# A set amount of other work between the steps of a recurrence (one encoder layer, one core)

## The chip, the core and the metric

The kernel runs on one core of a Trainium2 chip. The metric is the device time of one execution in microseconds (us). TensorE (PE in the profile) multiplies matrices, VectorE (DVE) and ScalarE (ACT) work on elements, GpSimd (POOL) does small row statistics and issues some DMAs, SyncE (SP) issues the others. Each engine runs its own queue of instructions in order, and waits on semaphores for the others.

## The reference

One layer of an encoder on 512 positions of width 1024, in three sub-layers: token mixing, cross-attention into 256 memory tokens, and a gated MLP with a short convolution. Each has a norm before and after it and is added to the residual. The change is in the token mixing, which has two groups of heads side by side: eight attention heads, and four heads of a gated recurrence in both directions over the positions. Shortened, the recurrence is:

```python
def hgrn2_group(q, zf_fwd, zf_bwd, i_in, g, lb, out_g):
    f = lb + (1 - lb) * sigmoid(z)          # a forget gate per direction and key column
    k = 1 - f                               # and S = diag(f_t) S + k_t v_t, o_t = q_t S
    o = bidirectional_gated_scan(silu(q), log(f_fwd), log(f_bwd), v=i_in)
    return rmsnorm(o, out_g) * silu(g)      # per head of 128
mixed = concatenate([attention, recurrence]) @ w_out
```

## The kernel before

**Matmuls.** Nearly all products are made from three matmuls (`mm3`, lines 278 to 280): each operand is split into a rounded high part and a rest. Activations are kept as such pairs (`big`), weights come through `issue`: a load into `raw`, a high part `wh` (L222, ScalarE), and a rest `wl` (L224 on VectorE, or L229 on ScalarE and an accumulating DMA L230 from GpSimd's queue). A unit of weights is 1024 columns, of 24 matmuls of 512 columns.

**The recurrence** of head h (`hgrn_core`) is not a scan over positions. It fills a 512 by 128 table of the scores of every pair of positions within a block, level by level for m = 1, 2, 4, ... 64: L644 copies the keys into order (`kc`), L647 multiplies keys and queries of neighbouring blocks of m, L679 puts the result in its place under a mask, and L673 scales keys and queries, in place, by the decay over m, for the next level. L678 forms the decays of the next level. L636 is the first product (a position with itself), with the sum of keys of L629. Then come m = 128 (L654, copied by L681), the transposed keys for the state (L659, copied by L660), the state (L664, copied by L666), and the output of the head (L685 to L687). L691 squares the output, L296 and L297 turn the sums into a row factor on GpSimd, L697 scales and gates the output, and L701 transposes it for the output projection. All products of the recurrence are of 128 columns, plain float32, which PE does in two passes (a transpose in one). They go to the two banks `ps_c`.

**Streams.** `hgrn_core` and the projections are generators. `weave` asks that stream for its next step which is furthest behind its share of work; a step is worth the number that it yields, in us by the author's count (`MM`, 0.216 for a matmul of 512 columns), and a stream that yields None is passed over. There are three weaves:

- before the first, the input, the values `v` and head 0's projection are made;
- the first, of `mix_projections` (100) and `cores` (53): output gate, then q and gates of head 1, of head 2 (L577 to L607), the transposes of the normed memory (L317), the attention's q, k and v (bank `ps_s` and `ps_o`; norm and rotation L725 to L750, and transposes L780 and L757), and q and gates of head 3; beside it the recurrence of heads 0, 1 and 2, one after the other;
- the second, of head 3's recurrence (22), attention (46; scores L872, transposes L882, weighing L893) and memory keys and values (52).

A projection yields after two slices of the contraction, 6 x 0.216 = 1.30; the recurrence yields 1.0 after each level, and 3.0 after the statistics. In the first weave the shares would give a recurrence step of 1.0 for each 1.89 of projections.

**Order on the engines.** The framework that builds the program puts instructions of one engine past others where it takes their inputs to be late; so rows that one loop writes together can stand apart in the order of an engine. All quoted line numbers are those of the kernel before; in the changed kernel they are 14 to 16 higher.

Of the kernel before, what the change touches and what calls it, by code (L numbers as in the profile page):

```python
# [47 lines left out]
NEG_SCALAR = frozenset(range(9, 33))  # L48
NEG_POOL = frozenset(range(33, 42))
CORE_SHARE, ATT_LEAD = 53.0, 4.0  # L50
KEY_TURNS = {1: (0, 1), 2: (2, 3)}
WARM, SPREAD_STEP = 4, 2
LEVELS = (1, 2, 4, 8, 16, 32, 64)
# [5 lines left out]
def pat(t, off, dims):  # L59
    a = t[:]  # L60
    return bass.AP(tensor=a.tensor, offset=a.offset + off, ap=[list(a.ap[0])] + [list(d) for d in dims])
# [8 lines left out]
        return self.hi[kc // n][:, kc % n, sl], self.lo[kc // n][:, kc % n, sl]  # L70


def weave(*streams):
    live = [[g, 0.0, float(total)] for g, total in streams]
    while live:
        live.sort(key=lambda s: s[1] / s[2])
        for s in live:
            try:
                step = next(s[0])
            except StopIteration:  # L80
                live.remove(s)
                break
            if step is not None:
                s[1] += step
                break
        else:
            raise RuntimeError("no stream can go on")


def layer(tc, io, out):  # L90
# [14 lines left out]
    def small():  # L105
        return sm.tile([P, 16], F32, name="small", tag="small")

    def bank(tag):
        return ps.tile([P, 512], F32, name="ps_" + tag, tag=tag)

    def big(shape, dt=F32):
        return b8.tile(shape, dt, name="big", tag="big")

    def tmp2(shape=(P, 512), dt=F32, tag="ta"):
        return t2.tile(list(shape), dt, name="tmp2", tag=tag, bufs=TMP_BUFS[tag])
# [8 lines left out]
    def split_scaled(hi, lo, src, factor):  # L124
        nc.scalar.mul(hi, src, factor)
        nc.vector.scalar_tensor_tensor(out=lo, in0=src, scalar=factor, in1=hi.bitcast(F32), op0=ALU.mult,
                                       op1=ALU.subtract)
# [154 lines left out]
    def blk(b):  # L282
        return slice(b * P, (b + 1) * P)
# [10 lines left out]
    def rstd_of(ss, n, width, r=None):  # L294
        r = small() if r is None else r
        nc.gpsimd.tensor_scalar(r[:, :n], ss, 1.0 / width, EPS, op0=ALU.mult, op1=ALU.add)  # L296
        last_pow[0] = nc.gpsimd.tensor_tensor(out=r[:, :n], in0=r[:, :n], in1=nhalf[:, :n], op=ALU.pow).ins  # L297
        return r
# [267 lines left out]
    def pair(act, i):  # L566
        t = big([P, 2, 2, T], F32R)
        act.hi[i], act.lo[i] = t[:, 0], t[:, 1]
# [49 lines left out]
    def hgrn_core(h):  # L618
        while h not in heads:
            yield None  # L620
        q, qk, tt = heads[h]
        room = big([P, 2048])
        a = room[:, 0:1024].rearrange("p (s w n) -> p s w n", s=NB, w=2)
        kt = room[:, 1024:1536].rearrange("p (s n) -> p s n", s=NB)
        st = room[:, 1536:1792].rearrange("p (g n) -> p g n", g=2)
        diag = a[:, :, 0, :]
        ksum, kc, qc = [tmp2(tag="th") for _ in range(3)]
        nc.scalar.mul(ksum, qk[:, 1, 0, :], oml[:, 0, h:h + 1])
        nc.vector.scalar_tensor_tensor(out=ksum, in0=qk[:, 1, 1, :], scalar=oml[:, 1, h:h + 1], in1=ksum,  # L629
                                       op0=ALU.mult, op1=ALU.add)  # L630
        for side, to in ((1, kc), (0, qc)):
            (nc.vector.tensor_copy if (h, side) == (1, 0) else nc.scalar.copy)(
                to, pat(qk, side * 2 * T, [[2, T // 2], [T + 1, 2]]))
        o = bank("c").rearrange("p (b n) -> p b n", b=NB)
        for b in range(NB):
            nc.tensor.matmul(o[:, b, :], ksum[:, blk(b)], q[:, blk(b)], start=True, stop=True)  # L636
        nc.scalar.copy(diag, o)
        yield 1.0
        toff = 0
        for i, m in enumerate(LEVELS + (128, 256)):  # L640
            if m <= 64:
                if m > 1:
                    kc = tmp2(tag="th")
                    nc.scalar.copy(kc, pat(qk, 2 * T, [[2 * m, T // (2 * m)], [T + m, 2], [1, m]]))  # L644
                o = bank("c").rearrange("p (b n) -> p b n", b=NB)
                for b in range(NB):
                    nc.tensor.matmul(o[:, b, :], kc[:, blk(b)], qc[:, blk(b)] if m == 1 else  # L647
                                     pat(qk, b * P, [[2 * m, P // (2 * m)], [T + m, 2], [1, m]]),
                                     start=True, stop=True)
            elif m == 128:  # L650
                o = bank("c").rearrange("p (b n) -> p b n", b=NB)
                for sb in range(NB):
                    tb = sb ^ 1
                    nc.tensor.matmul(o[:, sb, :], qk[:, 1, sb % 2, blk(sb)], qk[:, 0, tb % 2, blk(tb)],  # L654
                                     start=True, stop=True)
            else:
                o = bank("c").rearrange("p (b n) -> p b n", b=NB)
                for sb in range(NB):
                    nc.tensor.transpose(o[:, sb, :], qk[:, 1, sb // 2, blk(sb)], ident)  # L659
                nc.scalar.copy(kt, o)  # L660
                yield 0.5
                o = bank("c")[:, :256].rearrange("p (g n) -> p g n", g=2)
                for sb in range(NB):
                    nc.tensor.matmul(o[:, sb // 2, :], kt[:, sb, :], v[:, sb, blk(h)],  # L664
                                     start=sb % 2 == 0, stop=sb % 2 == 1)
                nc.scalar.copy(st, o)  # L666
                yield 1.0
                break
            nblk = T // m
            npair = nblk // 2  # L670
            for s, off, gap in ((1, 1, nblk - 1), (0, nblk + 1, -(nblk + 1))):
                c = pat(qk, s * 2 * T, [[2 * m, npair], [T + m, 2], [1, m]])
                nc.vector.tensor_tensor(out=c, in0=c, in1=pat(tt, toff + off, [[2, npair], [gap, 2], [0, m]]),  # L673
                                        op=ALU.mult)
            if m < 128:
                src = tt[:, toff:toff + 2 * nblk].rearrange("p (i two) -> p two i", two=2)
                toff += 2 * nblk
                nc.vector.tensor_mul(tt[:, toff:toff + nblk], src[:, 0, :], src[:, 1, :])  # L678
                nc.vector.copy_predicated(diag, masks[:, i:i + 1, :].to_broadcast([P, NB, P]), o)  # L679
            else:  # L680
                nc.scalar.copy(a[:, :, 1, :], o)  # L681
            yield 1.0
        o = bank("c").rearrange("p (b n) -> p b n", b=NB)
        for tb in range(NB):
            nc.tensor.matmul(o[:, tb, :], a[:, tb, 0, :], v[:, tb, blk(h)], start=True, stop=False)  # L685
            nc.tensor.matmul(o[:, tb, :], a[:, tb ^ 1, 1, :], v[:, tb ^ 1, blk(h)], start=False, stop=False)
            nc.tensor.matmul(o[:, tb, :], qk[:, 0, tb // 2, blk(tb)], st[:, 1 - tb // 2, :], start=False, stop=True)  # L687
        on = tmp2((P, NB, P), tag="th")
        ss = small()
        for b in range(NB):  # L690
            nc.scalar.activation(on[:, b, :], o[:, b, :], ACT.Square, accum_out=ss[:, b:b + 1])  # L691
        r = rstd_of(ss[:, :NB], NB, P)
        yield 3.0
        while len(sg_box) < 1 + NB:
            yield None
        for b in range(NB):
            nc.vector.scalar_tensor_tensor(out=on[:, b, :], in0=o[:, b, :], scalar=r[:, b:b + 1],  # L697
                                           in1=sg_box[0][:, b, blk(h)], op0=ALU.mult, op1=ALU.mult)
        o = bank("c").rearrange("p (b n) -> p b n", b=NB)
        for b in range(NB):  # L700
            nc.tensor.transpose(o[:, b, :], on[:, b, :], ident)  # L701
        if h % 2 == 0:
            pair(mix, 2 + h // 2)
        split_scaled(*mix.get(4 + h, slice(0, T)), o.rearrange("p b n -> p (b n)"), og[:, 0:1])
        rec_done[0] += 1
        yield 0.5
# [127 lines left out]
    def cores():  # L834
        for h in range(3):
            yield from hgrn_core(h)

    for i, _ in enumerate(hgrn_in(0)):
        if i == SPREAD_STEP:
            spread_r()  # L840
    weave((mix_projections(), 100.0), (cores(), CORE_SHARE))

    kT, vv, qT = qkv["kT"], qkv["vv"], qkv["qT"]
# [87 lines left out]
    def attention_filler():  # L931
        kv["k"] = Act([None] * 2, [None] * 2)
        for c in range(8):
# [3 lines left out]
            for step in proj_fm(kv["m"], M, "b", put_kx(c)):  # L937
                yield step
                turned[0] = c > max(KEY_TURNS)
            for b in KEY_TURNS.get(c, ()):  # L940
                turn_k(b)
# [150 lines left out]
    us = [bank(up_tags[n]) for n in range(4)]  # L1092
# [254 lines left out]
```

## Time and profile before

| | |
|---|---|
| median of 3 runs | 816.31 us (816.14 to 816.73) |
| span of the profiled execution, first to last instruction | 813.8 us |
| granted TensorE clock, mean | 0.998 |
| PE busy | 803.3 us, 99% of the span |
| PE weight loads | 691.0 us, 85% |
| DVE busy | 574.7 us, 71% |
| ACT busy | 482.1 us, 59% |
| POOL busy | 136.9 us, 17% |
| first weave, about | 54 to 200 us |
| second weave, about | 200 to 306 us |

The profile is of one execution; its span lies 2.5 us under the median of the runs, which hold what comes before the first and after the last instruction too. "Idle before" in brackets is the time that an engine stood still ahead of an instruction, with what it waited for. A row "x8" stands for eight instructions in a row. Busy time of PE includes modelled ends, so that two matmuls overlap in the list; the distance of their starts tells the pace.

### The profile page before, as it was taken

To read this page: it belongs to the slowest core of one execution; us is meant where nothing else is said; L and a number is where in the kernel's file an instruction comes from. 1 tells how busy PE (TensorE), PEld (TensorE's weight loads), DVE (VectorE), ACT (ScalarE), POOL (GpSimd) and SP (SyncE) were. 2 spreads that over 40 slices of the span, in tenths; PEclk is the share of its full clock that TensorE was granted. 3 is DMA by queue.
4 is the path that set the end of the run, shared out by engine and by line. 5 is a ranking of instruction groups with operands and counts; after the bars stand their busy time and mean duration, and the time that the engine had idled before them with its cause. 6 is when DMAs were issued, how large, how long until landed. Compare 5 with 4: busy or idle time off the path is not lost.

```text
span 813.8 us, 11771 instructions
## 1 busy us (share of the span) xinstructions
PE 803.3 (99%) x4426; PEld 691.0 (85%) x4426; DVE 574.7 (71%) x868; ACT 482.1 (59%) x796; POOL 136.9 (17%) x213
## 2 busy tenths in 40 slices
PE   9999999999999999999999999999999999999996
PEld 7888888889998887888888898899999998888885
DVE  5456587469886865855453767987777788888765
ACT  5675757459988874644543553665555545566651
POOL 0111201053233102301010311211111111000301
PEclk9999999999999999999999999999999999999999
DMA  8685645569899753256634158776665677278852
GB/s 296 202 259 139 160 103 117 118 159 247 229 250 254 182 172 126 78 181 157 180 117 142 33 164 208 154 200 166 179 171 143 150 200 178 91 208 278 239 130 104
DMA packets 42457, 139.61 MB, mean 172 GB/s; under 512 B 5280, under 2 KB 6560, under 8 KB 42400
## 3 DMA queue, kind: packets, MB, share of 16 engines
q1 hardware_dynamic: 28944, 97.43, 35.5%
q0 software_dynamic: 12160, 38.54, 26.2%
q10 hardware_dynamic: 1296, 2.89, 1.0%
q8 instruction: 34, 0.56, 0.3%
q14 instruction: 23, 0.19, 0.1%
HBM read 135.17 MB, written 25.17 MB: 197 GB/s over the span
## 4 chain that ended last, share of the span: by engine, by line
PE 92%; DVE 3%; ACT 2%; issue 1%; POOL 1%; DMA 0%; DVEq 0%; POOLq 0%; SPq 0%; ACTq 0%
PE ps_b L279 10%; PE ps_b L280 10%; PE ps_b L278 10%; PE ps_s L278 6%; PE ps_s L280 6%; PE ps_s L279 6%; PE ps_o L278 5%; PE ps_o L279 5%; PE ps_o L280 5%; PE ps_c L278 5%; PE ps_c L280 5%; PE ps_c L279 5%; PE ps_c L647 3%; PE ps_o L893 2%; PE ps_s L872 2%; PE ps_o L882 2%
## 5 line engine op out<-in xcount | busy, mean ns | idle before, releaser
L222 ACT CAST wh<-raw 128x1024 fp32r<-128x1024 f32 x110 | 113.7, 1035 | 114.6 <-PE ps_b L279 35.3
L224 DVE TENSOR_TENSOR wl<-raw,wh 128x1024 fp32r<-128x1024 f32 (+1 forms) x77 | 92.3, 1201 | 72.2 <-ACT wh L222 72.0
L278 PE MATMUL ps_b<-big,wh 128*128 128x512 f32 (+1 forms) x344 | 122.3, 355 | 0.0
L280 PE MATMUL ps_b<-big,wl 128*128 128x512 f32 (+1 forms) x344 | 121.2, 352 | 0.0
L279 PE MATMUL ps_b<-big,wh 128*128 128x512 f32 (+1 forms) x344 | 121.2, 352 | 0.0
L280 PEld LDWEIGHTS ps_b<-big,wl 128*128 128x128 f32 x344 | 65.1, 189 | 8.5 <-DMA wl<-in_wu_dram 0.2
L278 PEld LDWEIGHTS ps_b<-big,wh 128*128 128x128 f32 x344 | 65.1, 189 | 8.3
L279 PEld LDWEIGHTS ps_b<-big,wh 128*128 128x128 f32 x344 | 65.1, 189 | 8.1
L673 DVE TENSOR_TENSOR big<-big 128x512 f32<-128x512 f32 x64 | 47.2, 755 | 9.6 <-PE ps_c L647 4.0
L278 PE MATMUL ps_s<-wh,big 128*128 128x512 f32 (+1 forms) x140 | 53.4, 383 | 0.0
L279 PE MATMUL ps_s<-wl,big 128*128 128x512 f32 (+1 forms) x140 | 53.3, 381 | 0.0
L280 PE MATMUL ps_s<-wh,big 128*128 128x512 f32 (+1 forms) x140 | 53.0, 379 | 0.0
L230 POOL DMA_DIRECT2D wl<-in_w_dram x33 | 29.3, 887 | 126.7 <-ACT wl L229 91.5
L122 DVE TENSOR_TENSOR big<-ps_o,big 128x512 fp32r<-128x512 f32 x54 | 36.9, 687 | 15.0 <-ACT big L121 13.4
L121 ACT CAST big<-ps_o 128x512 fp32r<-128x512 f32 x54 | 31.7, 588 | 18.5 <-PE ps_o L996 7.5
L278 PE MATMUL ps_s<-big,wh 128*128 128x256 f32 (+1 forms) x120 | 40.0, 334 | 0.0
L279 PE MATMUL ps_s<-big,wh 128*128 128x256 f32 (+1 forms) x120 | 40.0, 333 | 0.0
L280 PE MATMUL ps_s<-big,wl 128*128 128x256 f32 (+1 forms) x120 | 40.0, 333 | 0.0
L278 PE MATMUL ps_o<-wh,big 128*128 128x512 f32 (+1 forms) x102 | 39.2, 385 | 0.0
L279 PE MATMUL ps_c<-big,wh 128*128 128x256 f32 (+1 forms) x120 | 39.1, 326 | 0.0
L278 PE MATMUL ps_c<-big,wh 128*128 128x256 f32 (+1 forms) x120 | 39.1, 326 | 0.0
L280 PE MATMUL ps_c<-big,wl 128*128 128x256 f32 (+1 forms) x120 | 39.1, 326 | 0.0
(315 smaller groups left out, 2149.3 us busy)
## 6 DMA issues: line engine op xcount, KB each, us to landing
raw<-in_w_dram SPq DMA_DIRECT2D x91, 512.0 KB, 3.6
wl<-in_w_dram POOLq DMA_DIRECT2D x33, 512.0 KB, 7.3
sum_t<-in_wd_dram SPq DMA_DIRECT2D x20, 512.0 KB, 6.3
tmp<-in_wu_dram SPq DMA_DIRECT2D x14, 512.0 KB, 6.9
sum_t<-in_wd_dram POOLq DMA_DIRECT2D x10, 512.0 KB, 8.4
sum_t<-sum_t POOLq DMA_DIRECT2D x10, 512.0 KB, 7.5
big<-sum_t SPq DMA_DIRECT2D x10, 512.0 KB, 4.7
raw<-sum_t SPq DMA_DIRECT2D x10, 512.0 KB, 4.4
```

The costliest lines, as they stand in the source:

```text
L121: nc.scalar.copy(hi, src)
L122: (eng or nc.vector).tensor_sub(lo, src, hi.bitcast(F32))
L222: nc.scalar.copy(wh, raw)
L224: last_low[0] = nc.vector.tensor_sub(wl[:, :by_dma], raw[:, :by_dma], wh[:, :by_dma].bitcast(F32)).ins
L230: nc.gpsimd.dma_start(wl[:, by_dma:], source(i)[:, by_dma:], accum_op=ALU.add)
L278: nc.tensor.matmul(o, a[0], b[0], start=start, stop=False, skip_group_check=again)
L279: nc.tensor.matmul(o, a[0], b[1], start=False, stop=False, skip_group_check=again)
L280: last_mm[0] = nc.tensor.matmul(o, a[1], b[0], start=False, stop=stop, skip_group_check=again).ins
L647: nc.tensor.matmul(o[:, b, :], kc[:, blk(b)], qc[:, blk(b)] if m == 1 else pat(qk, b * P, [[2 * m, P // (2 * m)], [T + m, 2], [1, m]]), st ...
L673: nc.vector.tensor_tensor(out=c, in0=c, in1=pat(tt, toff + off, [[2, npair], [gap, 2], [0, m]]), op=ALU.mult)
L872: nc.tensor.matmul(s, qT[h // 4][:, h % 4, blk(qb)], kT[:, 2 * (h // 4) + c, :], start=c == 0, stop=c == 1)
L882: nc.tensor.transpose(o[:, c, :], e[:, 0, blk(c)], ident)
```

## The change

A clock counts the work that `weave` hands out, of all streams. After the first inputs of a head and after each level up to m = 128 the recurrence yields None until that clock has gone on by a set amount, 3.0 or 2.0. If no stream can go on, the wait is dropped. The steps behind the levels (transposed keys, state, output, L697 to L701) have no such wait. Nothing is computed in another way.

```diff
+CORE_FIRST, CORE_STEP = 3.0, 2.0
...
+clock, stuck = [0.0], [False]
+
+
+def pace(us):
+    end = clock[0] + us
+    while clock[0] < end and not stuck[0]:
+        yield None
...
 def weave(*streams):
...
             if step is not None:
                 s[1] += step
+                clock[0] += step
+                stuck[0] = False
                 break
         else:
-            raise RuntimeError("no stream can go on")
+            if stuck[0]:
+                raise RuntimeError("no stream can go on")
+            stuck[0] = True
...
 def hgrn_core(h):
...
+        yield from pace(CORE_FIRST)
         o = bank("c").rearrange("p (b n) -> p b n", b=NB)
         for b in range(NB):
             nc.tensor.matmul(o[:, b, :], ksum[:, blk(b)], q[:, blk(b)], start=True, stop=True)
...
                 nc.scalar.copy(a[:, :, 1, :], o)
             yield 1.0
+            yield from pace(CORE_STEP)
```

What moves is seen in the order of instructions. The opening of head 1 on PE before, from its first product (L636) to the level m = 2 (the second L647); `ps_b` is a gate's projection:

```order
L636 MATMUL ps_c<-tmp_733,tmp_892 128x128 x4
L279 MATMUL ps_b<-big,wh 128x512
L280 MATMUL ps_b<-big,wl 128x512
L278 MATMUL ps_b<-big,wh 128x512
L647 MATMUL ps_c<-tmp_894,tmp_893 128x128 x4
L279 MATMUL ps_b<-big,wh 128x512
L647 MATMUL ps_c<-big,tmp_914 128x128 x4
```

There were three matmuls, then one, between these steps. Now (L651 is the L636 of before, L662 the L647, L292 to L294 are `mm3`):

```order
L651 MATMUL ps_c<-tmp_691,tmp_892 128x128 x4
L662 MATMUL ps_c<-tmp_894,tmp_893 128x128 x4
L292 MATMUL ps_b<-big,wh 128x512
L293 MATMUL ps_b<-big,wh 128x512
L294 MATMUL ps_b<-big,wl 128x512
L292 MATMUL ps_b<-big,wh 128x512
L293 MATMUL ps_b<-big,wh 128x512
L294 MATMUL ps_b<-big,wl 128x512
```

The row after these is again such a matmul: twelve stand between the two L662, and twelve between most later levels; the first product has moved behind the whole projection of 24.

The end of head 1 on PE before, the last rows of a gate's projection and the memory transposes (L317) ahead of the transposes of the head (L701):

```order
L280 MATMUL ps_b<-big,wl 128x512
L317 MATMUL ps_s<-ident,big 128x128 x4
L317 MATMUL ps_o<-ident,big 128x128 x4
L317 MATMUL ps_s<-ident,big 128x128 x4
L317 MATMUL ps_o<-ident,big 128x128 x4
L701 MATMUL ps_c<-ident,tmp_1073 128x128 x3
```

Between L687 and L701 stood 14 matmuls and these sixteen transposes. The same end now, from the last L687 (now L703) to the transposes (now L717), beside the q projection of the attention:

```order
L703 MATMUL ps_c<-big 128x128
L293 MATMUL ps_s<-wl,big 128x512
L294 MATMUL ps_s<-wh,big 128x512
L292 MATMUL ps_s<-wh,big 128x512
L293 MATMUL ps_s<-wl,big 128x512
L294 MATMUL ps_s<-wh,big 128x512
L292 MATMUL ps_o<-wh,big 128x512
L293 MATMUL ps_o<-wl,big 128x512
L294 MATMUL ps_o<-wh,big 128x512
L292 MATMUL ps_o<-wh,big 128x512
L717 MATMUL ps_c<-ident,tmp_1220 128x128
L293 MATMUL ps_o<-wl,big 128x512
```

Nine matmuls are left between the two, and the first of the four transposes stands alone. Head 0 ends in the same way; in head 2 there are 18 matmuls of 256 columns.

On ScalarE, at the memory transposes, before (L121 copies a bank of them out, L603 to L605 are a gate of head 2, L222 a weight cast):

```order
L222 CAST wh<-raw 128x1024
L121 CAST big<-ps_s 128x4x128
L603 ACTIVATE big<-tmp_1114 128x512
L604 ACTIVATE big<-tmp_1114 128x512
L605 ACTIVATE big<-big,lb,oml 128x512
L121 CAST big<-ps_o 128x4x128
```

And now, with L236 for L222, L617 to L619 for the gate and L135 for L121:

```order
L236 CAST wh<-raw 128x1024
L617 ACTIVATE big<-tmp_1039 128x512
L618 ACTIVATE big<-tmp_1039 128x512
L619 ACTIVATE big<-big,lb,oml 128x512
L135 CAST big<-ps_s 128x4x128
L135 CAST big<-ps_o 128x4x128
```

The gate has moved ahead of the first copy.

## The prediction

> **What bounds the kernel now.** I read four views in this order: the page, the busy time by stretch, the waits of TensorE's weight loads, and the timeline around single waits.
>
> ```profile
> PE 803.3 (99%) x4426; PEld 691.0 (85%) x4426; DVE 574.7 (71%) x868; ACT 482.1 (59%) x796; POOL 136.9 (17%) x213
> ```
> TensorE (PE) is the bound, so only what makes PE wait is worth time. A busy PE can hide a short wait, because the modelled end of a matmul reaches up to the next one. The weight loads (PEld) show the waits instead. In the stretch of the first weave, 54 to 180 us, they are these:
>
> ```profile
> PEld ps_c L647 <- ACT tmp L644: 2.5, 5, 1.0
> PEld ps_c L647 <- issue: 0.7, 2, 0.4
> PEld ps_c L647 <- ACT tmp L632: 0.7, 2, 0.4
> PEld ps_c L664 <- ACT big L660: 0.6, 2, 0.3
> PEld ps_c L654 <- DVE big L673: 0.6, 2, 0.3
> PEld ps_s L278 <- DVE big L122: 0.3, 1, 0.3
> PEld ps_c L636 <- DVE tmp L629: 0.2, 1, 0.2
> ```
> Columns: total us, times, longest. That is 5.6 us in 15 waits, nearly all in the recurrence (L636 to L664). So there is something for pacing to take back, but little. How much of it is lost PE time, two places show:
>
> ```profile
> 58.91 0.39 PE L280 MATMUL ps_s<-wh,big 128*128 128x512 f32 x1
> ...
> 59.14 0.39 PE L278 MATMUL ps_s<-wh,big 128*128 128x512 f32 x1
> ...
> 59.45 0.97 PEld L647 LDWEIGHTS ps_c<-big,tmp 128*128 128x128 f32 x8 [0.35 <-issue]
> 59.48 1.13 PE L647 MATMUL ps_c<-big,tmp 128*128 128x128 f32 x8
> ...
> 60.36 0.48 PE L279 MATMUL ps_s<-wl,big 128*128 128x512 f32 x1
> ...
> 61.82 1.05 PE L647 MATMUL ps_c<-big,tmp 128*128 128x128 f32 x8
> ...
> 62.63 0.48 PE L279 MATMUL ps_s<-wl,big 128*128 128x512 f32 x1
> ```
> ```profile
> 102.14 0.47 PE L279 MATMUL ps_b<-big,wh 128*128 128x512 f32 x1
> ...
> 103.30 1.02 PEld L647 LDWEIGHTS ps_c<-big,tmp 128*128 128x128 f32 x8 [1.00 <-ACT tmp L644]
> 103.33 1.20 PE L647 MATMUL ps_c<-big,tmp 128*128 128x128 f32 x8 [0.72 <-DVE big L673]
> ```
> A 512-column matmul takes 0.23 us from start to start (58.91 to 59.14). The level at 59.48 starts 0.34 after the matmul ahead of it, which is 0.11 late. From its start to the next matmul it needs 0.88, against 0.81 for the level at 61.82 that waits for nothing. So a wait shown as 0.35 costs about 0.2, and some 0.15 to 0.17 of each is free. The opening of head 1 costs 1.19 - 0.23 = 0.96, the largest single wait. In all, 5.6 - 15 x 0.17 = 3.0 us of PE time is lost there.
>
> **The change, part by part.** It adds no instruction, DMA or wait to any queue; it only moves the steps of the recurrence later among those of the projections.
>
> (A) Levels stand farther apart. The projections hand over work in steps of 6 x 0.216 = 1.30, so a pace of 2.0 means two such steps, twelve matmuls. The order now shows twelve between most levels, 12 x 0.23 + 0.9 = 3.7 us from level to level instead of about 2. The level chain (scaling on VectorE, copy on ScalarE) then fits without a wait. In head 0 two levels still stand four matmuls apart, and the copies ahead of L664 gain nothing: I keep 0.5 of the 3.0. A = -2.5 us. Ends: -3.0 (all go) and 0 (other waits take their place).
>
> (B) The end of a head moves close to its own statistics. Before, the step of 3.0 behind L691 was honoured, since the recurrence was up with its share. Paced, it is behind its share after every head's levels, so L697 and L701 are handed out at once. In the new order nine 512-column matmuls stand between the last L687 and the first L701 in heads 0 and 1, and 18 of 256 columns in head 2; before, there were 25 in head 0, 14 and sixteen transposes in head 1, and over sixty in head 2. What has to happen in between is measured:
>
> ```profile
> 123.43 0.39 PE L687 MATMUL ps_c<-big 128*128 128x128 f32 x2
> 123.86 0.28 ACT L691 ACTIVATE tmp<-ps_c 128x128 f32<-128x128 f32 x1 [1.42 <-PE ps_c L687]
> ...
> 125.09 0.19 POOL L296 TENSOR_SCALAR small<-small 128x4 f32<-128x4 f32 x1 [3.50 <-ACT tmp L691]
> 125.37 1.04 POOL L297 TENSOR_TENSOR small<-small,nhalf 128x4 f32<-128x4 f32 x1
> 126.44 1.13 DVE L697 SCALAR_TENSOR_TENSOR tmp<-ps_c,small,big 128x128 f32<-128x128 f32 x4 [3.21 <-POOL small L297]
> ```
> ```profile
> L701 PEldq EVENT_SEMAPHORE  x2: 51/51/51, 82.9 to 126.8; - x2
> ```
> From the start of the last L687 pair (123.43) the four squares, the power on GpSimd and the first of the four L697 take until 126.8, where PE's queue gets the signal (the last time in the row of L701): 3.4 us. PE's own work in that time is the pair (0.22) and nine matmuls (2.07), about 2.2 with the changeover between the two kinds. So PE stands for 3.4 - 2.2 = 1.2 us. The four transposes L701 now stand apart, with single matmuls between, and the third has to wait for its own quarter of L697: 0.1 more. Heads 0 and 1: 1.3 each. Behind L701 in PE's queue stand the next projections, which no other engine can take on, so this is lost in full.
>
> In head 2 the gap is 18 matmuls of half the width, at half of 0.23 again 2.07 us, but the chain runs in a stretch in which VectorE is packed:
>
> ```profile
> 125.00:171.00 46.00, 45.92 (x263) 39.15 (x263) 26.79 (x51) 25.83 (x46) 6.83 (x9) 1.00 0.53 117
> 171.00:206.00 35.00, 35.00 (x267) 33.11 (x266) 33.40 (x73) 30.78 (x52) 18.12 (x22) 1.00 0.85 230
> ```
> Columns: length; PE, PEld, DVE, ACT, POOL busy; clock; DMA. DVE is busy 33.4 of 35 us. GpSimd feels it:
>
> ```profile
> 186.33 0.62 POOL L296 TENSOR_SCALAR small<-small 128x8 f32<-128x8 f32 x1 [4.51 <-DVE small L727]
> ```
> L296 takes 0.62 here against 0.19 above, so I add 0.4: head 2 = 1.7. The Trainium skill (SBUF — State Buffer, "Who interferes with whom") says that a VectorE instruction with two SBUF inputs and a GpSimd one that reads SBUF exclude each other for a whole instruction. By that rule each of the two GpSimd steps could wait for one VectorE instruction of 0.6 us, and head 2 would be 1.3 + 1.2 = 2.5, the sum 0.8 higher; the trace shows only 0.4 in one step, and I go by that.
>
> B = +1.3 + 1.3 + 1.7 = +4.3 us. Low end 2.7 (0.9 a head, if the chain is as quick as its steps alone); high end 6.5, if ScalarE's squares of head 2 come behind the gates that the new order puts ahead of them (L603 to L605 and a weight cast, some 3 us).
>
> (C) The memory transposes (L317). In the new order ScalarE runs three gate instructions ahead of the first copy L121 out of that bank, for which the first q projection waits:
>
> ```profile
> 127.81 0.58 ACT L121 CAST big<-ps_s 128x512 fp32r<-128x512 f32 x1
> ...
> 128.28 0.63 ACT L603 ACTIVATE big<-tmp 128x512 f32<-128x512 f32 x1
> ...
> 130.04 0.57 ACT L121 CAST big<-ps_o 128x512 fp32r<-128x512 f32 x1
> ```
> The gates take 130.04 - 128.28 = 1.76 us; PE has one level (0.9) more to do meanwhile, and some of the copy's lead is lost in any case: C = +0.4 on top of the wait there now (ends 0 and +0.9).
>
> (D) From 180 to 212 us. The last levels, the state and the output of head 2 now stand in the packed stretch: two levels of 2 us and about 3.2 us of scaling and gating on VectorE, 7 us in all. In return the projections' own VectorE work arrives some 7 us earlier, because PE leaves 64 passes of head 2 (0.88 / 8 = 0.11 each) for later; VectorE was busy only 26.8 of 46 us ahead of the stretch, and that idle time is what hides it. If the cover fails, the key chain L727 to L750 is late next, and PE waits at the key transposes L757. Now PE waits there for
>
> ```profile
> PEld ps_c L647 <- ACT tmp L644: 0.7, 1, 0.7
> PEld ps_s L872 <- ACT big L758: 0.3, 1, 0.3
> ```
> A PE that comes 2 us later finds part of this done (-0.4); but the new order puts a weight pass (L229) ahead of L758, which the first scores need (+0.4). D = 0, with ends -1.0 (both waits go) and +2.5 (half of head 2's 7 us is not absorbed, less the 1 us now shown).
>
> Queues passed: SP's order is unchanged. GpSimd's L296 of heads 0 and 1 stands one weight DMA later, whose own input (L229) precedes the squares on ScalarE: nothing. In the second weave head 3 has a share of 22 to 98, slower than the pace asks for: nothing.
>
> Sum: -2.5 + 4.3 + 0.4 + 0 = +2.2 us. The profiled execution's span is 813.8, so 816.0; the median of the runs is 816.31, 2.5 us above that span, so the time is 818.5 us. Behind 306 us nothing changes, and PE-bound work passes a delay on whole.
>
> **Rivals.** 0.2% is 1.6 us, about what a measurement of this kernel can tell from no change.
>
> (R1) Same: the delay is absorbed later. PE arrives 2 us later at a stretch where it already waits 1.0 us in two places, and at others of the second weave; if VectorE and ScalarE use the gift, D is -1.0 and more, and A reaches 3.0: +0.7 us, 817.0. For it: these waits exist. Against: the same engines get head 2's work.
>
> (R2) Much slower: VectorE's queue stands still at L697 of head 2. It is in order, so while it waits some 3 us for GpSimd, the value and key work behind it (L126, L727 to L750) waits too, in a stretch with 1.6 us of slack. Then PE stands at L757 for the rest: +2 to +3 on the sum, 821. It decides if VectorE comes to L697 before the squares are done.
>
> (R3) Faster: B does not appear. If the nine matmuls cover the chain, only A and C are left, -2.1 us: 814.2. It needs the chain to be under 2.2 us, and it measured 3.4 with ScalarE, GpSimd and VectorE free.
>
> **How the numbers follow.** Forecast (+1.6 to +3.6): 0.42. R2: 0.13. R1, and whatever else ends within 1.6 us: 0.33. R3: 0.12. So slower 0.55, same 0.33, faster 0.12. The likeliest case alone reaches from 817.9 to 819.9. The range: below, A's end with B's low end and D's gain, -3.0 + 2.7 - 1.0 = -1.3, 815.0; above, R2, 821.3.
>
> **What would show it.** Right: the list of PEld waits loses most of its L647 rows and gains L701 <- DVE L697, three or more of 1 us each; the opening of head 1 shows no wait near 1 us. Wrong: no wait at L701, or waits of 2 us and more at L757, L647 or L872 behind 200 us. The sum fails first if the list shows new waits in the levels themselves.

## The result and the profile after

| | before | changed |
|---|---|---|
| median of 5 runs each, same chip | 816.31 us (815.76 to 816.73) | 819.35 us (818.08 to 820.38) |
| ratio, with its 95% interval | | 1.0037 (1.0025 to 1.0049) |
| span of the profiled execution | 813.8 us | 817.9 us (its time 819.67) |

The changed kernel is 3.0 us slower. The forecast was 818.5. The lines of the changed kernel are 14 to 16 higher: transposes of a head's end L717 (before L701), levels L662 (L647), key copy L774 (L758), first scores L888 (L872).

First the waits of TensorE's weight loads in the first weave, 54 to 185 us, after the change (total us, times, longest):

```profile
PEld ps_c L717 <- issue: 2.9, 2, 1.4
PEld ps_s L292 <- DVE big L136: 0.7, 1, 0.7
PEld ps_c L679 <- ACT big L675: 0.4, 2, 0.2
PEld ps_c L662 <- ACT tmp L659: 0.4, 1, 0.4
PEld ps_c L662 <- ACT wl L243: 0.3, 1, 0.3
PEld ps_c L662 <- DVE big L140: 0.3, 1, 0.3
PEld ps_c L703 <- ACT big L681: 0.2, 1, 0.2
```
Before, the recurrence's own waits were 5.3 us in 14 (all rows but that of the memory transposes); 1.6 us in six are left, L679, L662 and L703. In their place stands L717, twice. The row says "issue" because the weight load's queue holds the semaphore event; the matmul's own row names VectorE's L713. Its timeline in head 0:

```profile
86.36 0.39 PE L703 MATMUL ps_c<-big 128*128 128x128 f32 x2
...
86.79 0.28 ACT L707 ACTIVATE tmp<-ps_c 128x128 f32<-128x128 f32 x1 [2.59 <-PE ps_c L703]
...
88.31 1.04 POOL L311 TENSOR_TENSOR small<-small,nhalf 128x4 f32<-128x4 f32 x1
88.44 0.39 PE L294 MATMUL ps_b<-big,wl 128*128 128x512 f32 x1
...
89.38 1.12 DVE L713 SCALAR_TENSOR_TENSOR tmp<-ps_c,small,big 128x128 f32<-128x128 f32 x4 [5.67 <-POOL small L311]
...
89.88 0.31 PE L717 MATMUL ps_c<-ident,tmp 128*128 128x128 f32 x1 [1.05 <-DVE tmp L713]
...
91.05 0.40 PE L292 MATMUL ps_b<-big,wh 128*128 128x512 f32 x1
```
From the last pair of L703 to the first transpose 3.5 us pass, and the last matmul in between starts at 88.44. It needs 0.23, so PE loses 89.88 - 88.44 - 0.23 = 1.21 us. Worked out in the same way (last matmul, first transpose), head 1 loses 1.21 (143.43, 144.86) and head 2 1.10 (from 192.62 to 193.84, less 0.12).

Behind 185 us the longest waits are these:

```profile
PEld ps_s L888 <- ACT big L774: 2.0, 1, 2.0
PEld ps_o L909 <- DVE big L136: 1.7, 4, 0.9
PEld ps_c L717 <- issue: 1.1, 1, 1.1
...
PEld ps_c L651 <- ACT big L800: 0.4, 1, 0.4
```
Before, the first scores waited 0.3. Why it is 2.0 now, the chain of waits that ends there shows (start, us, what):

```profile
203.09 0.95 ACT wh L236
...
204.06 7.54 DMA raw<-in_w_dram
...
212.63 0.37 ACT big L135
212.99 0.95 ACT wl L243
213.95 0.97 ACT big L774 x2
...
214.97 1.20 PE ps_s L888 x4
```
ScalarE casts a weight (203.09), which frees the buffer for the next load (204.06). That load takes 7.54 us; ScalarE stands at its cast (L236) until it lands, and the key copy L774, whose input the second key transposes started at 210.32, is queued behind that cast and the weight pass L243. The same cast on ScalarE, first in the kernel before, with what followed it, then now:

```profile
209.38 1.05 ACT L222 CAST wh<-raw 128x1024 fp32r<-128x1024 f32 x1
210.59 1.07 ACT L758 CAST big<-ps_o 128x512 fp32r<-128x512 f32 x2
211.55 1.08 ACT L229 ACTIVATE wl<-wh 128x1024 fp32r<-128x1024 f32 x1
```
```profile
211.68 1.05 ACT L236 CAST wh<-raw 128x1024 fp32r<-128x1024 f32 x1 [1.97 <-DMA raw<-in_w_dram]
```
Before, the cast waited for nothing: its load was issued at 201.69 and took 6.7 us. And the key copy stood ahead of the weight pass, which now takes 0.96 us between the cast and the copy. The load comes late because the casts ahead of it do: before, ScalarE cast weights at 184.61, 190.49, 196.42 and 200.60, now at 189.73, 199.17 and 202.91. The stretches after the change (length; PE, PEld, DVE, ACT, POOL busy; clock; DMA share; GB/s), and behind them the second one before:

```profile
171.00:206.00 35.00, 33.83 (x277) 32.38 (x275) 30.76 (x68) 26.80 (x55) 13.70 (x20) 1.00 0.68 184
206.00:216.00 10.00, 8.18 (x67) 7.67 (x66) 6.11 (x16) 7.46 (x12) 2.30 (x3) 1.00 1.03 270
```
```profile
206.00:216.00 10.00, 9.34 (x73) 8.62 (x72) 7.97 (x17) 8.42 (x16) 2.14 (x3) 1.00 1.04 268
```
The stretch from 171 to 206 moved 230 GB/s before and 184 now. Behind 206 us the DMA engines are full in both kernels; what differs is how late the load is issued into that stretch.

### The profile page after: what moved, and what is told of

The parts are those of the page before. It is cut to its first block, busy times and chain, and to the rows that moved or that the text cites. A ratio compares the mean times of both kernels' runs of the same rounds, so it can differ in the third digit from the quotient of the medians.

```text
span 817.9 us, 11768 instructions
## 1 busy us (share of the span) xinstructions
PE 803.1 (98%) x4426; PEld 691.5 (85%) x4426; DVE 575.8 (70%) x868; ACT 482.1 (59%) x796; POOL 136.7 (17%) x213
## 4 chain that ended last, share of the span: by engine, by line
PE 74%; ACT 4%; DVE 2%; DMA 1%; issue 0%; POOL 0%; DVEq 0%; POOLq 0%; ACTq 0%
PE ps_b L294 7%; PE ps_b L293 7%; PE ps_b L292 7%; PE ps_s L293 6%; PE ps_s L294 6%; PE ps_s L292 6%; PE ps_o L292 5%; PE ps_c L292 5%; PE ps_c L293 5%; PE ps_c L294 5%; PE ps_o L293 4%; PE ps_o L294 4%; PE ps_o L909 1%; PE ps_s L888 1%; PE ps_o L898 1%; PE ps_c L662 1%
## 5 line engine op out<-in xcount | busy, mean ns | idle before, releaser
L236 ACT CAST wh<-raw 128x1024 fp32r<-128x1024 f32 x110 | 113.8, 1037 | 116.1 <-PE ps_b L293 34.7
L292 PE MATMUL ps_b<-big,wh 128*128 128x512 f32 (+1 forms) x344 | 122.6, 356 | 0.0
L294 PE MATMUL ps_b<-big,wl 128*128 128x512 f32 (+1 forms) x344 | 120.9, 352 | 0.0
L294 PEld LDWEIGHTS ps_b<-big,wl 128*128 128x128 f32 x344 | 64.9, 189 | 8.7
L292 PEld LDWEIGHTS ps_b<-big,wh 128*128 128x128 f32 x344 | 65.1, 189 | 8.0
L292 PE MATMUL ps_s<-wh,big 128*128 128x512 f32 (+1 forms) x140 | 53.5, 383 | 0.5 <-DVE big L136 0.5
L294 PE MATMUL ps_s<-wh,big 128*128 128x512 f32 (+1 forms) x140 | 53.1, 379 | 0.0
L136 DVE TENSOR_TENSOR big<-ps_o,big 128x512 fp32r<-128x512 f32 x54 | 37.0, 687 | 14.3 <-ACT big L135 14.2
L135 ACT CAST big<-ps_o 128x512 fp32r<-128x512 f32 x54 | 31.8, 589 | 17.7 <-PE ps_o L1012 7.5
L292 PE MATMUL ps_s<-big,wh 128*128 128x256 f32 (+1 forms) x120 | 40.0, 333 | 0.0
L294 PE MATMUL ps_s<-big,wl 128*128 128x256 f32 (+1 forms) x120 | 39.9, 332 | 0.0
L292 PE MATMUL ps_o<-wh,big 128*128 128x512 f32 (+1 forms) x102 | 39.1, 383 | 0.0
L292 PE MATMUL ps_c<-big,wh 128*128 128x256 f32 (+1 forms) x120 | 39.1, 325 | 0.0
L294 PE MATMUL ps_c<-big,wl 128*128 128x256 f32 (+1 forms) x120 | 39.0, 325 | 0.0
```

What stands on the lines that cost most here:

```text
L135: nc.scalar.copy(hi, src)
L136: (eng or nc.vector).tensor_sub(lo, src, hi.bitcast(F32))
L236: nc.scalar.copy(wh, raw)
L292: nc.tensor.matmul(o, a[0], b[0], start=start, stop=False, skip_group_check=again)
L294: last_mm[0] = nc.tensor.matmul(o, a[1], b[0], start=False, stop=stop, skip_group_check=again).ins
```

## The experiments

All ratios are to the kernel before, run on the same chip, with 95% intervals. That kernel's own median was 816.04 to 816.31 us beside these runs, so differences of a few tenths between two rows of the table say nothing.

| run | median us | ratio |
|---|---|---|
| x1: end of a head does not wait for its statistics | 814.59 | 0.9972 (0.9961 to 0.9982) |
| x2: CORE_STEP 1.0 | 813.64 | 0.9967 (0.9956 to 0.9978) |
| x3: first scores later | 823.82 | 1.0088 (1.0075 to 1.0102) |
| x4: before, ends at once | 821.75 | 1.0066 (1.0050 to 1.0082) |
| x5: opening paced only | 817.79 | 1.0018 (1.0009 to 1.0026) |
| x6: heads 0 and 1 paced only | 818.19 | 1.0025 (1.0014 to 1.0036) |
| x7: changed, copies early | 817.93 | 1.0022 (1.0013 to 1.0030) |
| x8: CORE_STEP 1.0, end paced 2.0 | 813.35 | 0.9965 (0.9953 to 0.9977) |
| x9: x8 with copies early | 813.53 | 0.9968 (0.9956 to 0.9981) |
| x10: before, copies early | 816.27 | 1.0001 (0.9992 to 1.0010) |
| x11: changed, end paced 4.0 | 816.01 | 1.0000 (0.9991 to 1.0009) |

**The price of the ends.** x1 takes away what the ends wait for: it leaves the norm of a head out of the result. On ScalarE the order is that of the changed kernel up to some 196 us:

```diff
-            nc.vector.scalar_tensor_tensor(out=on[:, b, :], in0=o[:, b, :], scalar=r[:, b:b + 1],
+            nc.vector.scalar_tensor_tensor(out=on[:, b, :], in0=o[:, b, :], scalar=nhalf[:, b:b + 1],
```


> The changed kernel, but the four gatings of a head's end (L713) multiply by a constant column instead of the power of the head's own statistics; squares and power still run, so only their use is left out. Nothing then stands between the last L703 and the transposes L717 but the gatings themselves. Theory (the ends of the heads cost 3.5 us: waits of 1.21, 1.21 and 1.10 at L717): the three waits go, the time falls by 3 to 3.5 us against the changed kernel's 819.35, to about 816, ratio to before 0.999 to 1.000. Rival (what is lost there is taken from later waits, at the first scores L888 above all): two waits go, but the time stays above 818, ratio 1.002 or more.

It fell by 4.8 us, more than the 3.5 expected. Up to 185 us two waits of 0.5 us in all are left at L717, and in head 2 none:

```profile
PEld ps_c L717 <- issue: 0.5, 2, 0.3
```
The wait at L888 is gone too, without being touched. So nothing that the ends lose is given back later: the rival falls. But the 4.8 are not the price of the ends alone. Behind 196 us ScalarE's order is another one here: no cast waits for its load, and L774 stands ahead of L243 and starts at 208.01, for scores at 209.16. That head 2's wait for its statistics brought on the wait at the scores is likely, but x1 does not show it apart from the new order.

x4 does the opposite: the kernel before, unpaced, with only the ends pulled near.

```diff
         r = rstd_of(ss[:, :NB], NB, P)
-        yield 3.0
+        yield 0.0
```


> The kernel before the change, unpaced, with only the 3.0 behind the statistics set to 0.0, so that each head's end is handed out at once: 11, 9 and 9 full-width matmuls between the last L687 and L701. Theory (a short distance there is the price, whatever put it there): waits at L701 of 0.8, 1.2 and 1.2 us, time 819.0 to 820.3, ratio 1.0033 to 1.005, nothing gained in the levels and the opening of head 1 still at about 1 us. Rival (the distance alone does not cost; the packed stretch and the shifted orders of the changed kernel do): 816.3 to 817.3, ratio under 1.0015.

5.4 us slower, where 3 to 4 were expected. The list of PEld's waits from 54 to 185 us begins so:

```profile
PEld ps_c L701 <- issue: 3.9, 3, 1.5
PEld ps_c L647 <- ACT tmp L644: 3.2, 7, 1.0
```
From start to start PE loses 0.82, 1.21 and 1.22 us at L701 in heads 0, 1 and 2, as expected. What the expectation left out is head 3 (0.67 more, at 267 us), the memory transposes that now meet a head's end (0.65, at 131 us), more level waits in head 2 (the row of L647 grew from 2.5 to 3.2) and 0.86 at the first scores instead of 0.30. So the 3.25 us at the ends of heads 0, 1 and 2 are the price of the distance alone, without pacing and ahead of the packed stretch.

**The gain of pacing.** x2 halves the pace between levels:

```diff
-CORE_FIRST, CORE_STEP = 3.0, 2.0
+CORE_FIRST, CORE_STEP = 3.0, 1.0
```


> The changed kernel with CORE_STEP 1.0 for 2.0: six matmuls between levels instead of twelve. The order then shows 24, 13 and 59 full-width matmuls between the last L703 and L717 of heads 0, 1 and 2, and head 2 is done before the packed stretch from 180 us, as before the change. Theory (the gain of pacing is real, 2.5 us, and its price comes only from how far twelve matmuls a level push the ends): no wait of 1 us at L717, level waits still under 1 us in all, opening of head 1 without a wait, first scores with at most 0.5 us; time 813.5 to 814.8, ratio 0.9965 to 0.998. Rival (pacing gains nothing that lasts; later stretches take it back): 816 or more, ratio 0.9995 or above.

813.64: faster than before by 2.7 us. The waits from 54 to 185 us:

```profile
PEld ps_c L662 <- ACT tmp L659: 2.2, 5, 0.7
PEld ps_c L679 <- ACT big L675: 0.8, 3, 0.3
PEld ps_c L717 <- DVE tmp L713: 0.6, 1, 0.6
PEld ps_c L662 <- issue: 0.3, 1, 0.3
```
One part of the expectation was wrong: the levels (L662) still wait 2.5 us by this list and the state (L679) 0.8, where under 1 was expected. Six matmuls between levels cover the chain of the levels only in part. The first scores wait 0.2. From 54 to 185 us all waits of the list went from 5.6 to 3.9 us; the rest of the 2.7 lies behind that, where among others a wait of 0.7 in a level and one of 0.8 at a projection are gone. So pacing by one projection step gains, and the recurrence is hardly ever so late that its ends lose their distance (0.6 at one transpose).

x8 adds the missing distance:

```diff
         yield 3.0
+        yield from pace(2.0)
```


> CORE_STEP 1.0 and a pace of 2.0 behind the statistics as well: 36, 18 and 59 full-width matmuls between the last L703 and L717 of heads 0, 1 and 2, and 60 and 18 ahead of the openings. Theory (with the ends far enough, the last wait at L717, 0.3 us in head 1, goes too): no wait at L717, time 0.2 to 0.6 us under the 813.64 of CORE_STEP 1.0 alone, ratio 0.996 to 0.9965. Rival (nothing left to gain there): 813.6 or more.

813.35, and no wait at L717 is left. The 0.3 us to x2 is less than the two intervals can tell apart. Both are the fastest versions here, 0.3% under the kernel before.

x5 paces only the opening (the line with CORE_STEP is taken out):

> Only the pace ahead of a head's opening (CORE_FIRST), none between the levels. Levels stand four to six matmuls apart as before the change; the ends keep 8 matmuls and the sixteen memory transposes (head 1) or more. Theory (the gain of the change has two parts, 0.96 us at the opening of head 1 and some 2 us in the levels): the opening's wait goes, the level waits stay, time 815.0 to 815.8, ratio 0.998 to 0.9995. Rival (the opening's wait is only handed to the next level): 816.3, ratio 0.9995 or more.

A miss: 817.8, slower than before. The opening's 0.96 became 0.66 at the next level, and head 1's end met the memory transposes:

```profile
PEld ps_c L662 <- ACT big L652: 0.7, 1, 0.7
...
PEld ps_c L716 <- DVE tmp L712: 0.6, 1, 0.6
PEld ps_s L292 <- DVE big L136: 0.5, 1, 0.5
```
VectorE does another step (L591, 0.6 us) between the second and the third of the four gatings (L712, one line higher here), so that the third transpose waits 0.6, and the next projection 0.5 for a copy (L136) behind the gatings. The rival was right: the wait is handed on, and a new one comes with the shift.

x11 keeps the step of 2.0 and paces the end alone, by `yield from pace(4.0)` behind the 3.0:

> The changed kernel, CORE_STEP still 2.0, with a pace of 4.0 behind the statistics: 18 and 17 full-width matmuls ahead of L717 in heads 0 and 1; head 2's levels and end go still deeper into the packed stretch, with 8 ahead of its L717. Theory (only near ends and a late head 2 cost): no wait at L717 of heads 0 and 1 (2.4 us and some 0.3 of single transposes back), about 1.2 left at head 2 and 1 to 2 us at the first scores; time 816.3 to 817.5, ratio 1.000 to 1.0015. Rival (a later head 2 costs more than the ends give): 818.5 or more.

816.01, a little under the expected range: 3.3 us back. In heads 0 and 1 the waits are gone; head 2 still loses 1.37 from start to start (the row reads 1.4), and instead of the first scores the key transposes wait:

```profile
PEld ps_c L718 <- issue: 1.4, 1, 1.4
PEld ps_o L774 <- ACT big L765: 0.8, 1, 0.8
```
So twelve matmuls a level, with far ends, just break even: the rest of their gain goes to a head 2 that ends in the packed stretch.

**The first scores.** x3 lets them in one key unit later:

```diff
-                turned[0] = c > max(KEY_TURNS)
+                turned[0] = c > max(KEY_TURNS) + 1
```


> The changed kernel with the attention's first scores (L888) let in one key unit later, 18 full-width matmuls behind the last key transposes instead of 6. Theory (the 2.0 us at L888 are PE waiting for the key copy L774, which stands on ScalarE behind a weight pass that waited for its DMA): the wait goes, no other takes its place, time 817.0 to 818.0, ratio 1.001 to 1.002. Rival (PE was early, and whatever it does there it meets the same DMA-paced weights a few us later): 819 or more, ratio 1.003 or above.

Wrong by 6 us, and beyond the rival: 823.8. The first scores wait for nothing now, but a level of head 3 took the wait over, and more:

```profile
PEld ps_c L662 <- ACT wh L236: 2.9, 1, 2.9
PEld ps_o L898 <- ACT tmp L874: 1.2, 1, 1.2
```
```profile
204.22 9.80 DMA raw<-in_w_dram
...
215.41 0.96 ACT wl L243
216.37 0.97 ACT big L774 x2
217.34 0.52 ACT tmp L659
```
The same load, issued at the same place, took 9.80 us instead of 7.54, and the copy that a level needs (L659) is in the same queue. What waits is ScalarE's whole queue, and moving one user of it only changes who meets the gap. By the lists, 2.9 at L662, 0.9 at a projection (216 us), 0.4 at a later score (L888) and 0.3 more at 254 us (1.2 for 0.9) are new, and the 2.0 at the first scores are gone: some 2.5 of the 4.5 us to the changed kernel. The rest is not assigned.

x7 acts on the load instead. Six copies of 512 KB and less (sum_t, L262), each issued beside a weight load, are moved three loads earlier; from 200 us on, the next copy is then issued at 211.16:

```diff
-SEEDS_AT = frozenset(range(28, 46)) | frozenset(range(60, 66))
+SEEDS_AT = frozenset(range(25, 31)) | frozenset(range(34, 46)) | frozenset(range(60, 66))
```


> The changed kernel with the copies of sum_t (L262), which are issued beside each weight load from 170 us on, moved so that three start earlier (from about 150 us) and none is issued between 200 and 212 us. Nothing is left out. Theory (the load issued at 204.06 lands at 211.60 because the DMA engines are full from 204 us on, and ScalarE's queue, with the key copy in it, waits for it): loads issued there land in 6 us or less, ScalarE does not wait for them, the wait at L888 falls from 2.0 to under 0.7 us; time 817.3 to 818.3, ratio 1.0012 to 1.0025; waits at L717 unchanged. Rival (ScalarE's own backlog sets it, not the load): the wait at L888 stays above 1.5 us, 819 or more.

As expected: 817.93, 1.4 us under the changed kernel (1.2 by the ratios; the two intervals overlap a little, so the times alone are a weak proof). The trace is the better one. ScalarE's wait for this load fell from 1.97 to 0.30 us. The chain to the first scores now reads

```profile
203.75 5.88 DMA raw<-in_w_dram
...
211.99 0.96 ACT big L774 x2
...
212.99 1.20 PE ps_s L888 x4
```
and the list has 0.6 at L888. So the load made 1.4 of the 2.0, not ScalarE's own backlog; the weight pass still stands ahead of the key copy. The control is x10, the same move in the kernel before:

> The kernel before the change, with only the sum_t copies moved in that way: a control for the same move in the changed kernel, where it gained 1.4 us. Theory (before the change no load was late there, and the waits of 0.7 at L647 and 0.3 at L872 have other causes): 815.6 to 816.6, ratio 0.9992 to 1.0006. Rival (the copies slow this stretch in any order, so that the gain says nothing about the pacing): 814.3 to 815.2, ratio under 0.9985.

No change (816.27), as expected: before the change no cast waited for a load there. The late load is the paced order's own.

x6 asks what makes it late. Heads 2 and 3 are not paced:

```diff
-            yield from pace(CORE_STEP)
+            if h < 2:
+                yield from pace(CORE_STEP)
```
(and so at the opening).

> The changed kernel with heads 2 and 3 not paced: heads 0 and 1 still end nine matmuls behind their statistics, head 2 runs its levels four matmuls apart and ends some 55 matmuls behind its own, ahead of the packed stretch, as before the change. Theory (the 2 us at the first scores come from head 2's end pushing ScalarE's weight casts back, so that loads bunch up in front of L888): waits of 1.2 us at L717 of heads 0 and 1, about 1 us of level waits in head 2, first scores with 0.5 us or less; time 816.3 to 817.5, ratio 1.000 to 1.0015. Rival (the delay of heads 0 and 1 alone makes it): the wait at L888 stays above 1.5 us, time 818.5 or more.

The mechanism held: 2.9 us at the ends of heads 0 and 1 (L719 here), and at the first scores

```profile
PEld ps_s L890 <- ACT big L776: 0.3, 1, 0.3
```
as before the change. So the delay of heads 0 and 1 does not make the 2.0. It comes with the pacing of head 2 or of head 3, whose opening stands in the same stretch; x6 takes both away, but x1 paces both and has no such wait. The time, 818.2, was 0.7 over the expected range: head 2's unpaced levels were priced too low (the waits for the copy alone are 2.0 us in five, against 0.4 in one in the changed kernel).

x9 joins x8, in which ScalarE still waited 1.03 us for a load, and the early copies:

> CORE_STEP 1.0, the pace of 2.0 behind the statistics, and the sum_t copies moved as in the run with the seeds early. Theory (there the ScalarE still waited 1.03 us for a load, while TensorE lost only 0.3 us at the first scores): that wait goes, TensorE gains 0 to 0.3 us; 812.9 to 813.5, ratio 0.996 to 0.9968. Rival (copies moved into an earlier stretch cost there): 814 or more.

Nothing gained: 813.53. ScalarE does not wait for a load any more, PE no longer waits at the first scores, and the time is that of x8 within the intervals.

## Why the prediction came out as it did

**What bounds the kernel.** Right. PE's busy share says nothing of the change (803.3 us before, 803.1 after); the list of PEld's waits showed each step.

**(A) Levels farther apart, -2.5.** Right in kind. By the prediction's own conversion (0.17 free of each wait) the 1.6 us in six waits that are left cost 0.6, and the 5.3 us in 14 before cost 2.9: -2.3. The opening of head 1 shows no wait. But no run prices A by itself. x2 bounds the net gain that pacing reached here at 2.7 us, some of it behind 200 us; and x5 shows that its largest piece, the opening, is worth nothing by itself.

**(B) Ends close to their statistics, +4.3.** This is the step that carried the forecast, and it held: 1.21, 1.21 and 1.10 us at the first transpose, where 1.2, 1.2 and 1.6 stood in the sum: 3.5 us. That the 1.2 was met to a hundredth is partly luck: the chain took 3.5 instead of 3.4, and PE's own work, for which the prediction put 2.2, was 2.3 (already its own 0.22 and 2.07 make 2.29). The 0.1 a head for transposes that stand single is not there: from the first transpose (89.88) to the first matmul behind the last (91.05) 1.17 us pass, for four transposes of 0.11 and three matmuls of 0.23, which are 1.13. And the surcharge of 0.4 in head 2 failed. GpSimd's two steps there ran as quickly as in head 0, at 88 us:

```profile
192.01 0.20 POOL L310 TENSOR_SCALAR small<-small 128x4 f32<-128x4 f32 x1 [9.29 <-ACT tmp L707]
192.30 1.01 POOL L311 TENSOR_TENSOR small<-small,nhalf 128x4 f32<-128x4 f32 x1
193.34 1.13 DVE L713 SCALAR_TENSOR_TENSOR tmp<-ps_c,small,big 128x128 f32<-128x128 f32 x4 [1.06 <-POOL small L311]
```
VectorE had nothing to do for 1.06 us of that time. The load of the stretch was read from the kernel before, where head 2's end was not in it. And the row read for it, L296 at 186.33, has 128x8 elements where a head's end has 128x4; two of the four rows of its shape in the stretch took 0.19 and 0.20 (179.87, 175.32). The Trainium skill's rule (SBUF — State Buffer, "Who interferes with whom"), by which the sum would have been 0.8 higher, had next to nothing to act on here; this trace says neither yes nor no to it.

x1 shows that the term was lost time, x4 and x11 that it belongs to the distance. The feared order of squares behind gates did not add to it: three gates and a cast stand ahead of head 2's squares, and the wait still was 1.10.

**(C) Memory transposes, +0.4.** Right: the row L292 <- L136 went from 0.3 to 0.7.

**(D) The packed stretch, 0, ends -1.0 and +2.5.** The mis-sized term. The level wait of 0.7 at L647 is gone, one of 0.4 at head 3's opening (L651) is new, and the first scores went from 0.3 to 2.0: +1.4 together. The prediction named the right instruction, L758 behind the weight pass L229, and priced that at 0.4, the half of one pass. It looked at compute queues alone. What it missed is the loop behind them: ScalarE's cast of a weight frees the buffer of the next load, in the paced order the casts come late (199.17 and 202.91 for 196.42 and 200.60), the DMA engines are less busy for a while (0.68 against 0.85), the load is issued late into a stretch in which they are full, and until it lands ScalarE's queue stands. The wait for the load (1.97) and the weight pass (0.96) stand one behind the other in the chain to the scores; x7 takes most of the first away, no run the second alone. The sign that the text gave for an error, waits of 2 us behind 200 us, did appear.

**The sum.** -2.3 + 3.5 + 0.4 + 1.4 = +3.0, the difference of the medians, against +2.2 forecast; each term is good to a few tenths only. D was forecast 1.4 too small and B 0.8 too large, so part of the two errors cancelled. The sum leaves out the waits behind 218 us (2.8 us in the list before, 3.3 after), so that it meets the medians to a tenth is chance. (The two profiled spans differ by 4.1. The changed kernel's lies 0.3 over the median of its five spans, 817.6; the 813.8 before lies 0.3 to 0.7 under that kernel's medians beside the experiments, 814.1 to 814.5. The rest is not resolved.)

**The rivals.** R1 (absorbed later) is refuted by x1: taking the waits away returned more than they cost. R2 had the right stretch and the wrong engine: VectorE reached L713 ahead of its input and stood 1.06 us, but nobody met that at the key transposes. R3 asked for a chain under 2.2 us; it was 3.5.

## What to carry to other kernels

A pace need not cover the whole chain that it hides, and what it adds is paid for at the end of the stream: one projection step per level, which left 3.3 us of waits in the recurrence, gained 2.7 us; two, which left 1.6, lost 3.0. A stream that falls behind its share loses every distance that was given to it as a share, so a slowed stream needs a set distance behind its last step too. And when work moves into a stretch that loads weights through few buffers, follow the buffer round: cast, release, load, cast.

## What the runs showed of the hardware

The same 512 KB weight load, issued within 0.5 us of the same moment (203.75 in x7, 204.06 in the changed kernel, 204.22 in x3) with the DMA engines about full (0.99 to 1.01 busy), took 5.88, 7.54 and 9.80 us; the 5.88 is the one without sum_t copies issued beside it. The Trainium skill (DMA: Bandwidth & Descriptors, "Queues, rings and completion order") says that each DMA engine goes round its queues packet by packet. That fits a load that slows beside the accumulating loads of GpSimd's queue; the sum_t copies are issued by SyncE like the weight loads themselves, so it does not by itself explain what they cost. The Trainium skill's fit for one transfer, given for GpSimd's path ("Anatomy of one DMA — SWDGE (gpsimd) path" on the same page), would make some 3.2 us for this size, an estimate. The loads that SyncE issued in the changed kernel at 190.79 and 200.28 came close to it with 3.1 us each; in the 1.8 us ahead of the second the DMA engines had been 0.05 busy. Why x3's load took 2.3 us longer than that of the changed kernel, with nearly the same loads beside it, is open.
